# An encoder layer's first stage: modulation by row sums, and two head pairs projected together

## The chip, the cores and the metric

The kernel runs on one core of a Trainium2 chip. TensorE (PE) multiplies matrices, VectorE (DVE), ScalarE (ACT) and GpSimd (POOL) work on tiles of 128 partitions, and SyncE (SP) issues the transfers. The metric is the device time of one execution in microseconds; the figure for a kernel is the median of several runs. A profiled execution of the same kernel shows where the time goes.

## The reference, cut to what matters

One layer of an encoder is computed: batch 1, 2048 tokens of 1024 features, 16 heads of 64. The mixer is stick-breaking attention, and a SwiGLU feed-forward part with 2816 hidden features follows. Everything is float32.

```python
mods = silu(c) @ ada_w + ada_b            # 6 x 1024: shift, scale, gate of the mixer, the same of the FFN
h = rms_norm(x, g) * (1 + scale) + shift  # the input of the mixer
q, k, v = h @ w_qkv                       # the projections, 16 heads each
z = q @ k.T * 64**-0.5                    # then softplus, reverse cumulative sums, exp: the weights a
o = (a @ v) @ w_o                         # the rest of the mixer, then the FFN in the same manner
```

The change concerns the first two and a half of these lines. Only `shift` and `scale` of the mixer are needed before the first projection, that is, the first 2048 of the 6144 columns of `ada_w` (8 MB).

## The kernel before, in words

**Tiles and precision.** The tokens are cut into 4 blocks of 512, the features into 8 tiles of 128 (`KC`), the heads into 8 pairs. A float32 product is made of three matmuls: each factor is split into a high and a low half, and `mm3` (L174 to L178) accumulates high by high (L176), high by low (L177) and low by high (L178). Such a group of three 128x512 matmuls is called a triple here; the projection of a pair and a block has 24 of them (k, q and v, by eight feature tiles), and its pieces are numbered t=1 (k), t=0 (q), t=2 (v) in the order in which they run.

**Steps.** `STEPS` lists the projections (pair, block). The first is (0,0); the second is the *parked* one, (1,0), whose keys, queries and values are stored to memory (`k_park`, `q_park`, `v_park`) and fetched again when pair 1 is due; then (0,1), (0,2) and so on. Attention of pair 0 on block 0 begins once (0,0) is projected and further projections run ahead: `SLICES` counts triples of each step, `AHEAD` says how many are done before the attention's slots begin, and `RATE` spreads the others over the slots.

**Order of work.** PE, ACT, DVE and POOL run in the order in which the program names their operations (`manual_schedule`). SP's order is set by a scheduler. On chip, tiles take turns in a few named groups of places (`ht`, `v`, `kt`, `whl`, `wraw` and so on, counts in `BUFS`), so a tile is loaded only when the tile that had its place has been read.

**The first stage.** The 8 MB of `ada_w` come in four quarters of 256 shift and 256 scale columns (`ada_chunk`). A quarter needs the sum over 1024 rows, each times its element of silu(c). DVE adds up most of the eight row tiles element by element (`ada_sum`: L724 for the first, L727 for each further one, 128x512), PE then sums over the partitions with matmuls against ones whose result is one column (`ada_rest`, L744), and one or two row tiles are multiplied on PE directly with c (`ada_direct`, L737, 128x1 results). `ada_cols_done` (L752 to L755) adds the bias and makes `shift` and `g_eff` = g·(1+scale). Each quarter serves two feature tiles.

Beside it, block 0 of x is squared (ACT, L167), its mean and root are taken (DVE L169, POOL L171), it is scaled (DVE, L341, 128x1024), and transposed feature tile by feature tile (PE, `x_turn`, L372, four 128x128 transposes a tile). `full_high` makes the modulated tile (ACT L782) and its high half (ACT L786), `low` its low half (DVE L791). Weights are split by `weights_high` (ACT L761) and `weights_low` (DVE L766). `first_products` then issues the three triples of a feature tile, for pair 0 alone.

```python
        first_products(m)
        if q < 3:
            turned_x[m + 2] = x_turn(0, m + 2)
            ada_direct(q + 1, KC - 1)
            if q == 0:
                first_products(m + 1, (1,))
            turned_x[m + 3] = x_turn(0, m + 3)
            ada_rest(q + 1)
```

**Block 1.** Blocks 1 and 3 are normalised by features: x comes already transposed from memory (`cols_load`, names `xc`), and what is missing is 1/rms of each token as a row. `x_square` and `x_spread` (L351 for the second) make it per token, `x_share` transposes it on PE (L363) and copies it (L365) to `x_row`. Then, for a feature tile k, `scale_cols` multiplies by that row (even k on DVE, L383; odd k on POOL, L387), and `modulate` makes high and low halves (even k: ACT L400, DVE L401; odd k: ACT L405 and L406, DVE L408). `first_norm` calls both; the scaling runs two tiles ahead. Before the change this lies beside the 24 triples of the parked step: `x_square` of block 1 in its t=1, `x_share` and two calls of `first_norm` in t=0, two more in t=2 (`NORM_AT`). Tiles 4 to 7 are normalised in t=1 of step (0,1), one ahead of each triple.

**Splits and turns.** Each finished projection is copied and split from its PSUM bank: high half by ACT (L507), low half by DVE (names kn and qn). Values are turned on PE (`values_turn`); for the first two steps this is put off, and done in t=1 of a later step (`waiting`). Block 2's x is squared at the places of `SQUARE_AT`, within t=0 and t=2 of the parked step.

Of the kernel before, what the change touches and what calls it, by code (L numbers as in the profile page):

```python
# [16 lines left out]
P = 128  # L17
# [22 lines left out]
SLICES = [0, 3 * KC] + [3 * KC + VGAP] * (NPAIR * NB - 2)  # L40


AHEAD = 6 * KC + 6
# [4 lines left out]

AQ = 256
# [25 lines left out]
SQUARE_AT = [(0, 2), (0, 7), (2, 1), (2, 7)]  # L75

NORM_AT = {
    None: [], 1: [(0, 4), (0, 6), (2, 3), (2, 5)],
    2: [(2, 2), (2, 4), (2, 6)], 3: [(2, 2), (2, 4), (2, 6)],
}  # L80
# [27 lines left out]
def hybrid_trunk_kernel(  # L108
# [5 lines left out]
    ada_first: bass.AP,  # L114
# [28 lines left out]
    shift = const.tile([P, 2, KC], F32, name="shift")  # L143
    c_act = const.tile([P, KC], F32, name="c_act")
# [19 lines left out]
    def rms_scale(pool, src, tag, junk):  # L164

        ssq = pool.tile([P, 1], F32, name=f"{tag}_ssq", tag="rms_ssq", bufs=10)
        nc.scalar.activation(junk, src, AF.Square, accum_out=ssq)  # L167
        ms = pool.tile([P, 1], F32, name=f"{tag}_ms", tag="rms_ms", bufs=4)
        nc.vector.tensor_scalar(ms, ssq, 1.0 / D, EPS, op0=ALU.mult, op1=ALU.add)  # L169
        rstd = pool.tile([P, 1], F32, name=f"{tag}_rstd", tag="rms_rstd", bufs=4)  # L170
        nc.gpsimd.tensor_tensor(rstd, ms, mhalf, op=ALU.pow)  # L171
        return rstd
# [33 lines left out]

    def split_early(p, t, tags):

        raw = raws.pop((p, t))
        if len(tags) == 1:  # L210
            hl = att.tile([P, 2, KC, P], F32R, name=f"w{p}_{t}", tag=tags[0], bufs=BUFS[tags[0]])
            hi, lo = hl[:, 0], hl[:, 1]
        else:
            hi, lo = [
                att.tile([P, KC, P], F32R, name=f"w{p}_{t}_{j}", tag=tag, bufs=BUFS[tag])
                for j, tag in enumerate(tags)
            ]
        nc.scalar.copy(hi, raw)
        nc.vector.tensor_tensor(lo, raw, f32(hi), op=ALU.subtract)
        weights[p, t] = hi, lo  # L220

# [85 lines left out]
    x_tiles, x_norm, x_rstd, x_cols, x_row = {}, {}, {}, {}, {}  # L307

    def x_load(b):
        for i in range(4):  # L310
            r0 = b * BT + i * P
            if b == 2:
                if i % 2 == 0:
                    pair = att.tile([P, 2, D], F32, name=f"x{b}_{i}", tag="qt", bufs=BUFS["qt"])
                tok = pair[:, i % 2]
# [5 lines left out]
    def cols_load(b):  # L321
        for m in range(KC // 2):
# [4 lines left out]
    def x_square(b, i):  # L327
        if b > 0:
# [5 lines left out]
            x_rstd[b, i] = rms_scale(att, tok, f"n0_{b}_{i}", junk=junk)  # L334
# [3 lines left out]
        x_rstd[b, i] = rms_scale(att, x_tiles[b, i], f"n0_{b}_{i}", junk=xn)  # L338
# [38 lines left out]
    def scale_cols(b, k):  # L377
# [4 lines left out]
        if k % 2 == 0:  # L382
# [6 lines left out]
    def modulate(hl, b, k):  # L389

        gain, add = g_eff[:, 0, k : k + 1], shift[:, 0, k : k + 1]
# [7 lines left out]
        if k % 2 == 0:  # L399
# [18 lines left out]
    norm_h, norm_tile = {0: []}, {}  # L418

    def first_norm(b, k):  # L420
# [9 lines left out]
        if k % 2 == 1:  # L430
            nc.sync.dma_start(h_s[b][:, k - 1 : k + 1], f32(norm_tile[b]))
# [21 lines left out]
    def project(at):  # L453

        p, b = STEPS[at]
        begun = (p, b) == (0, 0)
# [7 lines left out]
        def product(t):  # L464
            if begun:
                return first_acc[t]
            w = weights[p, t]
            if parked and t == 1:
                acc = zps.tile([P, BT], F32, name=f"pj{p}_{b}_{t}", tag="z")
            else:  # L470
                acc = accps.tile([P, BT], F32, name=f"pj{p}_{b}_{t}", tag="acc")
            ahead = b == NB - 1 and p + 1 < NPAIR
            for k in range(KC):
                if t == 1:
# [4 lines left out]
                    if k == 5 and waiting:  # L479
                        waiting.pop()()  # L480
                if parked and t == 1 and k % 2 == 0:
                    nc.sync.dma_start(*stores[k // 2])
                if parked and (t, k) == (1, 6):
                    split_early(1, 2, ["whl"])
                if nb in (1, 3) and t == 1 and k < 4:
                    x_square(nb, k)
                if nb and t == 1 and 2 <= k < 6:
                    x_spread(nb, k - 2)
# [6 lines left out]
                if (t, k) in NORM_AT[nb]:  # L495
                    first_norm(nb, NORM_AT[nb].index((t, k)))
# [8 lines left out]
        def split(acc, tag):  # L505
            hl = att.tile([P, 2, BT], F32R, name=f"{tag}n{p}_{b}", tag="qkn", bufs=BUFS["qkn"])
# [25 lines left out]
        if parked:  # L532
            nc.sync.dma_start(q_park, f32(n))
        else:
# [7 lines left out]

# [154 lines left out]
    chunks, piece_sums, cols_ps = {}, {}, {}  # L697

    ON_PE = {0: (0, KC - 1), 1: (KC - 1,), 2: (KC - 1,), 3: (KC - 1,)}

    def ada_chunk(q, kh):
        ks = range(KC // 2 * kh, KC // 2 * (kh + 1))
        if q == 2:
            for k in ks:
                w = att.tile([P, 2, AQ], F32, name=f"ac{q}_{k}", tag="a", bufs=BUFS["a"])
                nc.sync.dma_start(w, ada_first[q, kh][:, :, k % 4])
                chunks[q, k] = w
            return
        tag = "ht" if (q, kh) == (1, 1) else "qt"
        w = att.tile([P, 2, KC // 2, AQ], F32, name=f"ac{q}_{kh}", tag=tag, bufs=BUFS[tag])  # L710
        nc.sync.dma_start(w, ada_first[q, kh])
        for k in ks:
            chunks[q, k] = w[:, :, k % 4]

    def ada_begin(q):
        cols_ps[q] = zps.tile([P, BT], F32, name=f"acol{q}", tag="z")
        nc.vector.memset(cols_ps[q][:, :4], 0.0)

    def ada_sum(q, k):
        w, scale = chunks[q, k], c_act[:, k : k + 1]  # L720
        if q not in piece_sums:
            acc = att.tile([P, 2, AQ], F32, name=f"asum{q}", tag="w", bufs=BUFS["w"])
            piece_sums[q] = acc
            nc.vector.tensor_scalar(acc, w, scale, None, op0=ALU.mult)  # L724
        else:
            acc = piece_sums[q]
            nc.vector.scalar_tensor_tensor(acc, w, scale, acc, op0=ALU.mult, op1=ALU.add)  # L727

    def ada_sums(q):
        return [k for k in range(KC) if k not in ON_PE[q]]  # L730

    COLUMNS = [(2 * seg + j, seg, slice(j * P, (j + 1) * P)) for seg in range(2) for j in range(2)]

    def ada_direct(q, k):

        for n, seg, js in COLUMNS:
            nc.tensor.matmul(  # L737
                cols_ps[q][:, n : n + 1], chunks[q, k][:, seg, js], c_act[:, k : k + 1],
                start=False, stop=False, skip_group_check=True,
            )  # L740

    def ada_rest(q):
        for n, seg, js in COLUMNS:
            nc.tensor.matmul(  # L744
                cols_ps[q][:, n : n + 1], piece_sums[q][:, seg, js], ones[:, 0:1],
                start=False, stop=n == 3, skip_group_check=True,
            )

    def ada_cols_done(q):

        ps, ms = cols_ps.pop(q), slice(2 * q, 2 * q + 2)
        nc.vector.tensor_tensor(shift[:, 0, ms], ps[:, 0:2], b_cols[:, 0, ms], op=ALU.add)  # L752
        sc = att.tile([P, KC], F32, name=f"sc0_{q}", tag="sc", bufs=1)[:, :2]
        nc.vector.tensor_tensor(sc, ps[:, 2:4], b_cols[:, 1, ms], op=ALU.add)
        nc.vector.scalar_tensor_tensor(  # L755
            g_eff[:, 0, ms], sc, 1.0, gc[:, 0, ms], op0=ALU.add, op1=ALU.mult
        )

    def weights_high(t):
        hl = att.tile([P, 2, KC, P], F32R, name=f"w0_{t}", tag="whl", bufs=BUFS["whl"])  # L760
        nc.scalar.copy(hl[:, 0], raws[0, t])  # L761
        weights[0, t] = hl[:, 0], hl[:, 1]

    def weights_low(t):
        hi, lo = weights[0, t]
        nc.vector.tensor_tensor(lo, raws.pop((0, t)), f32(hi), op=ALU.subtract)  # L766

    def first_products(m, ts=(1, 0, 2)):
        for t in ts:
            w = weights[0, t]  # L770
            mm3(
                first_acc[t], (w[0][:, m], w[1][:, m]),
# [3 lines left out]
    def full_high(m):  # L776
        if m % 2 == 0:
            ht = att.tile([P, 2, 2, BT], F32R, name=f"ht0_0_{m // 2}", tag="ht", bufs=BUFS["ht"])
            first_h.extend([ht[:, 0], ht[:, 1]])
            norm_tile[0] = ht  # L780
        full = att.tile([P, BT], F32, name=f"hf0_{m}", tag="tmp", bufs=BUFS["tmp"])
        nc.scalar.activation(  # L782
            full, turned_x.pop(m), AF.Identity,
            bias=shift[:, 0, m : m + 1], scale=g_eff[:, 0, m : m + 1],
        )
        nc.scalar.copy(first_h[m][:, 0], full)  # L786
        first_full[m] = full

    def low(m):
        hl = first_h[m]  # L790
        nc.vector.tensor_tensor(hl[:, 1], first_full.pop(m), f32(hl[:, 0]), op=ALU.subtract)  # L791
        if m % 2 == 1:
            stores.append((h_s[0][:, m - 1 : m + 1], f32(norm_tile[0])))

    nc.sync.dma_start(c_act, c)
    nc.scalar.activation(c_act, c_act, AF.Silu)

# [914 lines left out]
```

## Time and profile before

| what | value |
|---|---|
| runs | 2847.48, 2847.53 and 2849.8 us, median 2847.53 us |
| the profiled execution's own time | 2847.32 us |
| its span, from the first to the last recorded instruction | 2845.3 us |
| busy in the span: PE | 2797.2 us (98%) |
| busy in the span: DVE, ACT, POOL | 2025.0 (71%), 1634.2 (57%), 1288.2 us (45%) |

The profile's page gives busy times of the engines, the span in 40 slices, the chain of waits that ended last, and groups of instructions by line. In such a line the parts are: line of the program, engine, operation, output<-inputs, shapes and types, count (x), then busy time, mean ns of one, idle time ahead of them and what ended it. A timeline row is the start in us, the length in us, and what ran. In the windows each row is one stretch: its bounds and length, the busy us (and count) of PE, PE's weight loads, DVE, ACT and POOL, the granted clock of TensorE (1.00 is full), the mean busy share of the transfer engines, and GB/s.

### The profile page before, as it was taken

To read this page: it belongs to the slowest core of one execution; us is meant where nothing else is said; L and a number is where in the kernel's file an instruction comes from. 1 tells how busy PE (TensorE), PEld (TensorE's weight loads), DVE (VectorE), ACT (ScalarE), POOL (GpSimd) and SP (SyncE) were. 2 spreads that over 40 slices of the span, in tenths; PEclk is the share of its full clock that TensorE was granted. 3 is DMA by queue.
4 is the path that set the end of the run, shared out by engine and by line. 5 is a ranking of instruction groups with operands and counts; after the bars stand their busy time and mean duration, and the time that the engine had idled before them with its cause. 6 is when DMAs were issued, how large, how long until landed. Compare 5 with 4: busy or idle time off the path is not lost.

```text
span 2845.3 us, 41773 instructions
## 1 busy us (share of the span) xinstructions
PE 2797.2 (98%) x13825; PEld 2335.3 (82%) x13825; DVE 2025.0 (71%) x2824; ACT 1634.2 (57%) x3275; POOL 1288.2 (45%) x2036
## 2 busy tenths in 40 slices
PE   8999999999999999999999999999999999999998
PEld 6788888888888888887888788888788888888887
DVE  6788898888888888888866766655776655133376
ACT  5787777788777877777645533333433333322233
POOL 1475666666575655657410122221222222544454
PEclk9999999999999999999999999999999999999999
DMA  9865547657565635646289644334453335545566
GB/s 359 291 219 167 189 151 231 210 170 235 182 211 193 202 123 179 201 127 236 80 304 313 207 137 152 123 94 161 134 175 110 111 105 166 191 139 154 181 212 200
DMA packets 240520, 521.04 MB, mean 183 GB/s; under 512 B 22448, under 2 KB 110512, under 8 KB 222640
## 3 DMA queue, kind: packets, MB, share of 16 engines
q1 hardware_dynamic: 240304, 518.38, 56.1%
q8 instruction: 109, 1.79, 0.3%
q14 instruction: 107, 0.88, 0.1%
HBM read 351.04 MB, written 118.49 MB: 165 GB/s over the span
## 4 chain that ended last, share of the span: by engine, by line
PE 85%; DVE 5%; issue 3%; ACT 2%; POOL 2%; DMA 2%; SPq 0%; DVEq 0%; POOLq 0%; ACTq 0%
PE s L176 9%; PE s L177 9%; PE s L178 9%; PE z L604 8%; PE o L683 8%; PE t L655 8%; PE pj L176 5%; PE pj L177 5%; PE pj L178 5%; PE o L178 4%; PE o L177 4%; PE o L176 4%; PE y L178 2%; PE y L176 2%; PE y L177 2%
## 5 line engine op out<-in xcount | busy, mean ns | idle before, releaser
L645 POOL TENSOR_TENSOR a<-a,w 128x512 f32<-128x512 f32 (+3 forms) x640 | 621.1, 970 | 225.3 <-DVE w L638 130.4
L638 DVE TENSOR_TENSOR_SCAN w<-z,c,begin 128x512 f32<-128x512 f32 x384 | 489.4, 1279 | 84.7 <-ACT z L623 62.1
L176 PE MATMUL s<-r,l 128*128 128x512 f32 x1232 | 481.8, 391 | 4.8 <-DVE p L1447 3.9
L178 PE MATMUL s<-r,l 128*128 128x512 f32 x1232 | 479.9, 389 | 0.0
L177 PE MATMUL s<-r,l 128*128 128x512 f32 x1232 | 479.8, 389 | 0.0
L621 ACT ACTIVATE a<-z 128x512 f32<-128x512 f32 (+3 forms) x640 | 347.1, 542 | 170.7 <-PE z L604 137.6
L683 PE MATMUL o<-aT,v 128*128 128x512 f32 (+3 forms) x1280 | 384.8, 382 | 0.1
L671 DVE TENSOR_TENSOR aT<-t,aT 128x512 fp32r<-128x512 f32 (+3 forms) x640 | 358.8, 595 | 23.7 <-ACT aT L665 23.1
L604 PE MATMUL z<-kt,qt 128*128 128x512 f32 (+3 forms) x1280 | 363.8, 366 | 0.1
L665 ACT CAST aT<-t 128x512 fp32r<-128x512 f32 (+3 forms) x640 | 314.0, 533 | 73.8 <-PE t L655 63.7
L623 ACT ACTIVATE z<-z 128x512 f32<-128x512 f32 (+3 forms) x640 | 345.5, 540 | 0.0
L1455 POOL TENSOR_TENSOR one<-p,p 128x512 f32<-128x512 f32 x44 | 71.5, 1624 | 576.7 <-issue 320.3
L176 PE MATMUL pj<-ht,w 128*128 128x512 f32 x768 | 309.5, 403 | 5.0 <-issue 1.4
L655 PE MATMUL t<-begin,a 128*128 128x128 f32 x2176 | 295.9, 274 | 14.1 <-DVE aT L671 12.9
L655 PEld LDWEIGHTS t<-begin,a 128*128 128x128 f32 x2176 | 255.5, 140 | 64.8 <-DVE aT L671 15.6
L177 PE MATMUL pj<-ht,w 128*128 128x512 f32 x768 | 303.7, 395 | 1.8 <-DVE ht L408 0.6
L178 PE MATMUL pj<-ht,w 128*128 128x512 f32 x768 | 303.3, 395 | 0.0
L176 PEld LDWEIGHTS s<-r,l 128*128 128x128 f32 x1232 | 231.3, 188 | 54.8 <-ACT l L1308 2.9
L178 PEld LDWEIGHTS s<-r,l 128*128 128x128 f32 x1232 | 231.3, 188 | 48.1
L177 PEld LDWEIGHTS s<-r,l 128*128 128x128 f32 x1232 | 231.4, 188 | 47.9 <-issue 0.5
L633 DVE TENSOR_TENSOR_SCAN w<-z,begin 128x128 f32<-128x128 f32 (+3 forms) x256 | 208.8, 818 | 77.0 <-ACT z L623 66.3
L604 PEld LDWEIGHTS z<-kt,qt 128*128 128x128 f32 x1280 | 230.6, 189 | 37.8 <-DVE w L633 0.5
(179 smaller groups left out, 4881.6 us busy)
## 6 DMA issues: line engine op xcount, KB each, us to landing
ht<-h_s SPq DMA_DIRECT2D x108, 1024.0 KB, 8.5
wi<-in_win SPq DMA_DIRECT2D x86, 512.0 KB, 4.0
qt<-qn SPq DMA_DIRECT2D x124, 256.0 KB, 4.9
ol_qt<-act_s SPq DMA_DIRECT2D x56, 512.0 KB, 3.9
act_s<-S SPq DMA_DIRECT2D x66, 256.0 KB, 3.9
br<-in_wout SPq DMA_DIRECT2D x66, 256.0 KB, 3.5
h_s<-ht SPq DMA_DIRECT2D x16, 1024.0 KB, 8.3
o_s<-os SPq DMA_DIRECT2D x128, 128.0 KB, 3.0
```

Of the source, the lines that this page charges most:

```text
L176: nc.tensor.matmul(acc, lhs[0], rhs[0], start=first, stop=False, **kw)
L177: nc.tensor.matmul(acc, lhs[0], rhs[1], start=False, stop=False, **kw)
L178: nc.tensor.matmul(acc, lhs[1], rhs[0], start=False, stop=last, **kw)
L604: nc.tensor.matmul(z[:, :n], q[:, e, part, r * P : (r + 1) * P], k[:, e, :n], start=part == 0, stop=part == 1,)
L621: nc.scalar.activation(a[:, :n], z[:, :n], AF.Sigmoid, scale=QK_SCALE)
L623: nc.scalar.activation(z[:, :n], z[:, :n], AF.Sigmoid, scale=-QK_SCALE)
L638: nc.vector.tensor_tensor_scan(rest[:, rev], left[:, rev], begin[:, :BT][:, rev], initial=carries[r], op0=ALU.mult, op1=ALU.bypass,)
L645: nc.gpsimd.tensor_tensor(a[:, :n], a[:, :n], rest[:, 1 : n + 1], op=ALU.mult)
L655: nc.tensor.transpose(pt[:, rb * P : (rb + 1) * P], weighed[i, rb][:, j * P : (j + 1) * P], ident)
L665: nc.scalar.copy(hl[:, 0, t0:], pt[:, t0:])
L671: nc.vector.tensor_tensor(hl[:, 1, t0:], pt[:, t0:], f32(hl[:, 0, t0:]), op=ALU.subtract)
L683: nc.tensor.matmul(acc[:, t0:], lhs, hl[:, part, t0:], start=sc == qb and j == 0 and part == 0, stop=sc == 0 and j == 3 and part == 1,)
```

## The change

The first stage is written anew; the code from the attention's units on stays as it is.

- **Modulation.** `ada_w` is laid out by feature tile (m = 0 to 7, one half each for shift and scale, 128x1024 each). For m = 0 and 1 (`COLUMNS`) PE makes the column by eight matmuls of 128x1 (`column`). For m = 2 to 7 the transposed rows are loaded, and one DVE instruction multiplies 128x1024 by silu(c) on all partitions and sums along the row (`row_sum`). silu(c) is put on all partitions by two matmuls against ones (`c_over`) and two copies (`c_copy`). `row_done` adds the bias, for one feature tile at a time.
- **Both pairs.** The triples of pair 1 on block 0 (the parked ones) run together with those of pair 0, feature tile by feature tile; pair 1 accumulates in the banks of `zps`. Both steps' products lie in the first stage, `SLICES` is 0 for both.
- **One list.** `FIRST` orders all operations of PE, ACT, DVE, POOL, and the issue of some loads and stores of SP. An entry is a name and its numbers: `sum.ms` half s of tile m, `mod.m` `row_done`, `sq`/`ms`/`sc`.bi square, mean and scaling of x, `xT.m`, `full.m`, `high.m`, `low.m`, `wh`/`wl`.pt the weight halves, `p.ptm` a triple, `sp`/`row` block 1's `x_spread`/`x_share`, `norm.k` `first_norm` of block 1, `c`/`cr` silu(c), `d.` loads and stores.
- **Block 1** is normalised by DVE and ACT alone (odd k too). `norm.0` and `norm.1` stand near the end of the list, calls 2 and 3 come with the splits of step (0,0), 4 to 7 in t=1 of (0,1) as before.
- **Places and SP.** The parked keys and queries are split into places of `wraw` instead of `qkn`; the first two stores of block 1's h wait (`held`) until the parked queries are stored; raw weights of pair 1 load into `v`. Squares of block 2 move to t=0 of (0,1), four in a row; the two waiting turns of values come at k=3 and k=5 of its t=1, oldest first.

The diff, cut to its core:

```diff
+COLUMNS = 2
-SLICES = [0, 3 * KC] + [3 * KC + VGAP] * (NPAIR * NB - 2)
-AHEAD = 6 * KC + 6
+SLICES = [0, 0] + [3 * KC + VGAP] * (NPAIR * NB - 2)
+AHEAD = 3 * KC + 6
...
-        if k % 2 == 0:
+        if k % 2 == 0 or b == 1:
             nc.vector.scalar_tensor_tensor(
                 u, u, g_eff[:, 0, k : k + 1], x_row[b], op0=ALU.mult, op1=ALU.mult
             )
...
-            nc.sync.dma_start(h_s[b][:, k - 1 : k + 1], f32(norm_tile[b]))
+            out_of = h_s[b][:, k - 1 : k + 1], f32(norm_tile[b])
+            if b == 1 and k < 4:
+                held.append(out_of)
+            else:
+                nc.sync.dma_start(*out_of)
...
-        begun = (p, b) == (0, 0)
+        begun = at < 2
...
             if begun:
-                return first_acc[t]
+                if at == 0 and t != 2:
+                    first_norm(1, 2 + (t == 0))
+                return first_acc[p, t]
...
-                    if k == 5 and waiting:
-                        waiting.pop()()
+                    if k in (3, 5) and waiting:
+                        waiting.pop(0)()
...
-                if nb == 1 and (t, k) in SQUARE_AT:
-                    x_square(2, SQUARE_AT.index((t, k)))
+                square_at = {2: 0, 3: 1}.get(nb)
+                if t == square_at and k < 4:
+                    x_square(nb, k)
+                    x_mean(nb, k)
...
         def split(acc, tag):
-            hl = att.tile([P, 2, BT], F32R, name=f"{tag}n{p}_{b}", tag="qkn", bufs=BUFS["qkn"])
+            place = "wraw" if parked else "qkn"
+            hl = att.tile([P, 2, BT], F32R, name=f"{tag}n{p}_{b}", tag=place, bufs=BUFS[place])
...
+    def column(m, seg):
+        w = rows[m][seg].rearrange("p (k f) -> p k f", f=P)
+        out_col = acol[:, 2 * m + seg : 2 * m + seg + 1]
+        for k in range(KC):
+            nc.tensor.matmul(
+                out_col, w[:, k], c_act[:, k : k + 1], start=k == 0, stop=k == KC - 1,
+            )
+
+    def row_sum(m, seg):
+        w = rows[m][seg]
+        if m not in sums:
+            sums[m] = att.tile([P, 2], F32, name=f"as{m}", tag="as", bufs=3)
+        nc.vector.scalar_tensor_tensor(
+            w, w, 1.0, c_rows, op0=ALU.mult, op1=ALU.mult, accum_out=sums[m][:, seg : seg + 1]
+        )
+
+    def row_done(m):
+        total = acol[:, 2 * m : 2 * m + 2] if m < COLUMNS else sums.pop(m)
+        nc.vector.tensor_tensor(mod[:, :, m], total, b_cols[:, 0:2, m], op=ALU.add)
+        nc.vector.scalar_tensor_tensor(
+            g_eff[:, 0, m : m + 1], mod[:, 1, m : m + 1], 1.0, gc[:, 0, m : m + 1],
+            op0=ALU.add, op1=ALU.mult,
+        )
...
+    nc.sync.dma_start(c_act, c)
+    row_load(0)
+    nc.sync.dma_start(c_line[0:1], c_row)
+    x_load(0)
     nc.sync.dma_start(b_cols, ada_b_cols)
     nc.sync.dma_start(gc, g_cols)
+    row_load(1)
+    load_weights(0, 1)
     load_weights(0, 0)
-    load_weights(0, 2, "qkn")
+    load_weights(0, 2, "kt")
+    row_load(2)
+    for t in (1, 0, 2):
+        load_weights(1, t, "v")
+    for m in (3, 4, 5):
+        row_load(m)
...
+    FIRST = """
+        sum.00 sq.00 sum.01 ms.00 sq.01 sq.02 ms.01 sc.00 sq.03 ms.02 sc.01 c mod.0 wh.01 ms.03
+        sc.02 wh.00 wl.01 wh.02 sc.03 d.rows wl.00 xT.0 cr sum.10 wl.02 full.0 high.0 sum.11 sum.20
+        low.0 xT.1 xT.2 mod.1 p.000 sum.21 wh.11 p.010 mod.2 p.020 wh.10 wl.11 full.1 p.110 wl.10
+        full.2 xT.3 high.1 xT.4 sum.30 p.100 high.2 wh.12 low.1 low.2 p.001 p.011 sum.31 p.021 wl.12
+        d.x1a d.xc0 p.101 d.xc1 d.xc2 d.st0 p.111 mod.3 sum.41 p.120 p.121 sum.40 full.3 p.002 p.012
+        high.3 sum.51 p.022 p.102 low.3 p.112 mod.4 p.122 sum.50 p.003 mod.5 p.013 full.4 sum.61
+        p.023 sq.10 p.103 sum.60 d.x1b d.st1 d.x2 high.4 p.113 p.123 sq.11 low.4 xT.5 mod.6 ms.10
+        p.004 full.5 ms.11 sum.71 p.014 sq.12 p.024 sp.10 sp.11 high.5 p.104 ms.12 sum.70 sq.13
+        p.114 p.124 low.5 d.st2 xT.6 ms.13 sp.12 p.005 full.6 mod.7 p.015 sp.13 high.6 p.025 low.6
+        p.105 p.115 p.125 xT.7 d.xc3 p.006 full.7 p.016 high.7 p.026 low.7 d.st3 p.106 p.116 p.126
+        p.007 p.017 p.027 row.1 p.107 p.117 norm.0 norm.1 p.127
+    """
```

More of the change, by code (lines that the diff above doesn't have):

```diff
@@ L47 @@
 EAGER = 12
-AQ = 256
 BUFS = {
@@ new lines, in hybrid_trunk_kernel @@
+    for n in range(4):
+        moves[f"xc{n}"] = lambda n=n: cols_load(1, n)
+        moves[f"st{n}"] = lambda n=n: store(n)
+    begin_do = {
+        "sum": lambda m, seg: (column if m < COLUMNS else row_sum)(m, seg),
+        "mod": row_done, "sq": x_square, "ms": x_mean, "sc": x_scale, "sp": x_spread, "row": x_share,
+        "xT": turn_x, "full": full, "high": high, "low": low, "wh": weights_high, "wl": weights_low,
+        "p": lambda p, t, m: products(p, m, t), "norm": lambda k: first_norm(1, k),
+        "c": c_over, "cr": c_copy,
+    }
```

316 lines of the change are left out of this document (120 added, 196 removed).

## The prediction

> **What bounds the kernel now.** I read the page first, then the windows of the first 160 us, then the timelines of PE, ACT and DVE there, then the groups by form.
>
> ```profile
> span 2845.3 us, 41773 instructions
> PE 2797.2 (98%) x13825; PEld 2335.3 (82%) x13825; DVE 2025.0 (71%) x2824; ACT 1634.2 (57%) x3275; POOL 1288.2 (45%) x2036
> 2.60:20.70 18.10, 8.33 (x33) 6.82 (x33) 9.97 (x19) 9.66 (x16) 3.38 (x4) 1.00 0.98 397
> 20.70:34.20 13.50, 13.42 (x43) 10.97 (x43) 11.25 (x22) 4.25 (x6) 0.00 (x0) 1.00 1.05 387
> 56.50:77.90 21.40, 20.66 (x95) 16.28 (x94) 16.02 (x29) 17.73 (x31) 11.10 (x12) 1.00 1.01 369
> 118.90:160.00 41.10, 34.83 (x178) 27.38 (x177) 34.06 (x44) 35.00 (x74) 33.79 (x54) 0.96 0.62 207
> ```
>
> PE is busy for 2797.2 of 2845.3 us, so whatever PE does not spend, or spends at half clock, is the only thing to win. In the windows (columns: length, then busy PE, PEld, DVE, ACT, POOL, then clock, DMA share, GB/s) PE works 8.33 us of the first 18.10, then nearly always; the next real hole is at 118.9 to 160, 6.3 us, far behind the edit. The DMA share is about 1 at 387 to 397 GB/s, so nothing can be fetched earlier: what is needed first must be asked for first.
>
> ```profile
> 20.70 0.79 PE L176 MATMUL pj<-ht,w 128*128 128x512 f32 x1 [0.67 <-ACT ht L786]
> 22.60 0.63 PE L176 MATMUL pj<-ht,w 128*128 128x512 f32 x1
> 23.02 0.63 PE L177 MATMUL pj<-ht,w 128*128 128x512 f32 x1
> 25.16 1.06 PE L372 MATMUL xT<-begin,xn 128*128 128x128 f32 x4
> 26.00 1.71 PE L737 MATMUL acol<-c_act,ac 128*128 128x1 f32 x8
> 27.57 0.78 PE L176 MATMUL pj<-ht,w 128*128 128x512 f32 x1
> 34.12 0.44 PE L176 MATMUL pj<-ht,w 128*128 128x512 f32 x1
> 35.34 0.39 PE L178 MATMUL pj<-ht,w 128*128 128x512 f32 x1
> 35.56 0.39 PE L176 MATMUL pj<-ht,w 128*128 128x512 f32 x1
> 36.25 0.60 PE L372 MATMUL xT<-begin,xn 128*128 128x128 f32 x4
> 36.69 0.95 PE L737 MATMUL acol<-c_act,ac 128*128 128x1 f32 x8
> 77.25 0.50 PE L177 MATMUL pj<-ht,w 128*128 128x512 f32 x1 [0.28 <-DVE ht L408]
> 77.81 0.39 PE L176 MATMUL pj<-ht,w 128*128 128x512 f32 x1
> ```
>
> Products begin at 20.70 and follow each other every 0.427 us (22.60 to 23.02). From 34.12 they follow every 0.2275 us (35.34 to 35.56). The clock column shows 1.00 all along, yet everything on PE halves there: four transposes 0.84 then 0.44, eight passes of a 128x1 matmul 1.57 to 1.71 then 0.8. So 13.4 us of products ran at half speed. A 128x1 matmul is two passes here (four instructions, eight records): cold about 0.43 us each. At 77.81 step (0,1) begins its second product (t=0); from there both kernels run the same list, so I compare that instant: **before, 77.81**.
>
> **When the first product starts.** Ahead of the first weights the changed kernel fetches row 0, x, row 1: 1.05+2.1+1.05 MB. Before, it was 4.2 MB too, so the weights land as they do now, at 15.24, and the next at 16.63.
>
> ```profile
> 15.24 1.05 ACT L761 CAST w<-wr 128x1024 fp32r<-128x1024 f32 x1 [0.19 <-DMA wr<-in_wqkv]
> 16.63 1.04 ACT L761 CAST w<-wr 128x1024 fp32r<-128x1024 f32 x1 [0.34 <-DMA wr<-in_wqkv]
> 19.22 0.78 ACT L782 ACTIVATE hf<-xT,shift,g_eff 128x512 f32<-128x512 f32 x1 [1.54 <-PE xT L372]
> 20.02 0.62 ACT L786 CAST ht<-hf 128x512 fp32r<-128x512 f32 x1
> 60.30 0.59 ACT L365 COPY x<-xr 128x512 f32<-128x512 f32 x1 [0.38 <-PE xr L363]
> L766 DVE TENSOR_TENSOR w<-wr,w 128x1024 fp32r<-128x1024 f32 x3 | 3.6, 1222 | 0.1
> L727 DVE SCALAR_TENSOR_TENSOR asum<-ac,c_act,asum 128x512 f32<-128x512 f32 x23 | 17.3, 750 | 1.0 <-DMA ac<-in_ada_first 0.4
> L791 DVE TENSOR_TENSOR ht<-hf,ht 128x512 fp32r<-128x512 f32 x8 | 5.5, 690 | 2.5 <-ACT ht L786 2.2
> L755 DVE SCALAR_TENSOR_TENSOR g_eff<-sc,gc 128x2 f32<-128x2 f32 x4 | 0.6, 161 | 0.1
> L341 DVE TENSOR_SCALAR xn<-x,n_rstd 128x1024 f32<-128x1024 f32 x4 | 3.0, 750 | 0.5 <-POOL n_rstd L171 0.4
> ```
>
> In the listed order DVE does wl.01 ahead of sc.03: 15.24+1.05+1.22+0.75 = 18.3, and only then can PE end xT.0. Behind xT.0 on PE stand sum.10 and sum.11, 16 matmuls of 128x1, 32 passes, four rows like 26.00's: 4x1.71 = 6.8 us. Row 1 has landed long before (ahead of 15.24), but the place in the list is behind xT.0, so PE does them at 18.3 to 25.1. Then xT.1 and xT.2, 2x0.84: **first product at 26.8 instead of 20.70**. Nothing covers this: the third weights land at 16.63+0.52/0.397 = 17.9, and ACT has high.0 ready at 17.9+1.05+2x0.59 (cr, as L365)+0.78+0.62 = 21.5, DVE low.0 near 22.2. The early columns sum.00 and sum.01 cost nothing: PE is idle before 18.3, as the 8.33 busy of 18.10 shows. What goes are 36 such matmuls: 12 stood before the first product, the other 24 between the products, 2x1.57 cold + 4x0.8 warm = 6.3 us. About as much as comes in front; the start eats the gain.
>
> **From there to the last product.** Up to p.027 PE has 45 triples, 135 products, 135x0.2275 = 30.7, seven xT and the row transposes, 8x0.44 = 3.5; together 34.2 us at full clock, counted from 25.1. When the clock turns I bound by the one full dip the trace has:
>
> ```profile
> 128.21 0.33 PE L655 MATMUL t<-begin,a 128*128 128x128 f32 x1 [2.28 <-DVE aT L671]
> 129.00:131.00 2.00, 1.98 (x11) 1.44 (x11) 1.76 (x5) 1.53 (x4) 1.51 (x4) 0.69 0.87 279
> 131.00:133.00 2.00, 2.00 (x9) 1.84 (x9) 1.54 (x2) 0.59 (x2) 1.77 (x7) 0.50 0.00 0
> 133.00:135.00 2.00, 2.00 (x13) 1.64 (x12) 0.58 (x1) 1.20 (x2) 1.37 (x2) 0.95 0.00 0
> ```
>
> After a wait of 2.28 us the clock is 0.5 for 1.2+2.0+0.2 = 3.4 us, all busy, then full: decisions come in steps of 3.4 us. At the start no step turned it while columns stood between the products (26.00 to 27.57, and once more); it turned 2.7 us after the last columns. So I count columns as idle and let the clock turn after the first full step of transposes and products from 25.1: between 27.9 and 31.3, I take 29.6. The 4.5 cold us do the work of 2.4: 25.1+34.2+2.1 = 61.4. With the copy of L365 x_row stands at 62.1.
>
> The Trainium skill, "TensorE: Matmul & The Clock Gate", section "What's actually happening", has the clock rise after about 3.4 us of sustained activity. The dip agrees; the 13.4 us at the start do not unless columns count for little.
>
> Can DVE keep up? A row sum, scalar_tensor_tensor of 128x1024 with accumulation, isn't in the trace. The next rows are 1.22 (L766, same size, two tensors) and 0.75 for half the size (L727, same operation). The size costs 0.53 per 512 (1.22-0.69), so 0.75+0.53 = 1.28; I take 1.3. From 20.3 (wl.02 done) to low.5 DVE has 12 sums 15.6, three wl 3.7, six lows 4.1 and some 18 small steps like L755, 3.0: ready by 47 if nothing waits; the listed order makes it wait for sq.12 behind full.5, so about 50. PE reaches low.5 near 50.4 (m=0 to 4 done). Slack under 1 us there, about 5 us at low.3 and low.4, 2 us at low.6 and low.7. sq.13 stands on ACT before full.6 and waits for the fourth x tile, about 18.4 MB into the queue: 2.6+18.4/0.397 = 49; needed by 50.3. On SP the third x1 tile waits for wl.12 and the fourth for sum.60, and st1, x2, st2, xc3, st3 stand behind; nobody needs those before 62. Six row tiles as sums take 12x1.3 = 15.6 of DVE where it spent 28 pieces, 17.3+1.9: off the path either way.
>
> **Step (0,1).** This is the price of doing two pairs together: before, block 1 was normalised beside the 72 products of the parked pair. Now norm.0 starts with x_row, and no product is left to hide it but nine.
>
> ```profile
> L383 DVE SCALAR_TENSOR_TENSOR xc<-xc,g_eff,x 128x512 f32<-128x512 f32 x4 | 2.9, 743 | 0.0
> 62.04 1.41 DVE L383 SCALAR_TENSOR_TENSOR xc<-xc,g_eff,x 128x512 f32<-128x512 f32 x2
> 68.78 0.74 DVE L383 SCALAR_TENSOR_TENSOR xc<-xc,g_eff,x 128x512 f32<-128x512 f32 x1
> 69.44 0.75 DVE L401 SCALAR_TENSOR_TENSOR ht<-xc,shift,ht 128x512 fp32r<-128x512 f32 x1
> L401 DVE SCALAR_TENSOR_TENSOR ht<-xc,shift,ht 128x512 fp32r<-128x512 f32 x4 | 3.8, 951 | 0.3 <-ACT ht L400 0.2
> 78.01 0.59 ACT L507 CAST kn<-pj 128x512 fp32r<-128x512 f32 x1 [1.30 <-PE pj L178]
> ```
>
> Back to back these follow every 0.66 us (68.78 to 69.44). All eight tiles now go by DVE: 8 scalings, 8 low halves, and between them four splits kn, qn, kn, qn (0.61, as L791 less the same overlap): 16x0.66+4x0.61 = 13.0, the last low done at 62.1+13.2 = 75.3. PE ends p.127 near 63.6. It cannot start k=0 before the first kn frees its bank, which stands ninth in DVE's order: 62.1+8x0.66+0.69 = 68.1. So PE stands 4.5 us, drops to half clock by the dip above and turns up a step after it restarts: three triples cold 3.8, a turn of values 0.8, five triples and a turn warm 3.9. t=1 ends at **76.6**. By the mean of L401 (0.95, where POOL multiplies beside it) the chain is 2 us longer; POOL no longer does, so I take 0.66 and keep 2 us for the range. The squares of block 2 moved to t=0 of this step: four of 1.05 on ACT behind kn end at 82, the last scaling at 83.8, where xT of block 2 is wanted at 83.5: 0.3 us lost. The order of SP from here on is as before; the parked stores move less than 8 MB between 68 and 90, which 0.4 MB/us carries before x of block 3 is squared.
>
> **Sum.** 76.6+0.3 against 77.81: -0.9 us. The profiled execution took 2847.32 (span 2845.3 and 2.0 around it), the median of the runs is 2847.53; so **2846.5**. 0.2% is 5.7 us, about what a measurement of this kernel can tell from no change.
>
> **Rivals.**
> *Row sums at half rate* (slower). If accumulation makes DVE read one tensor per cycle, a sum costs 4x0.53+0.22 = 2.35 us. PE takes 4.1+0.44 us for one tile of both pairs, DVE two sums and 1 us: it becomes the bound above 1.75 us a sum. Then low.5 comes at 20.3+12x2.35+10.8 = 59.3, and PE needs 11.1 us from there to the end of the row transposes (two tiles 8.2, three triples 2.05, two turns 0.9): 70.4 for 61.4, with the -0.9 +8.1 us: 2855.6. For it: no row has this operation with accumulation. Against: L727 reads two fp32 tensors at 0.75 per 512, barely over L791's 0.69. The Trainium skill, "Vector Engine (DVE) Microarchitecture Reference", section "Points that are easy to get wrong", says that this operation with two non-bf16 SBUF sources runs at half throughput; L727 disagrees without accumulation.
>
> *Columns warm the clock* (faster). Then PE turns during sum.10, by about 22.7, the rest of the columns takes half and the products never run cold: 24.0+34.2 = 58.2, 3.2 us earlier, -4.1 us: 2843.4; without the dip at 129.8 too (3.4 us at half, 1.6 lost), 2841.8. Against: 26.00 to 27.57.
>
> *The clock stays low as long as before*, 13.4 us from the first product, to 40.2: 10.6 us more at half, +4.9, so +4.0: 2851.5.
>
> **How the numbers follow.** Forecast 0.56, of which its tails give 0.05 faster and 0.03 slower (stalls on DVE or a longer norm chain, -4 to +4); half rate 0.15 (0.13 slower); warm columns 0.18 (0.10 over 5.7 us faster, with the dip gone); long cold 0.11 (0.03 slower, with other stalls). Faster 0.15, slower 0.19, same 0.66. The range reaches to the faster and the slower rival, 2841.8 to 2855.6, leaving out the ends beyond.
>
> **What would show it.** First product at 26.8 with 6.8 us of 128x1 passes in front; row sums of 1.3 us; PE without gaps from 25 to 63; x_row at 62; a hole of 4 us on PE then, with the clock at 0.5; (0,1)'s t=0 from 76.6. Wrong if products start near 22, if a sum takes 2 us, or if PE stands before p.005.

## The result, and the profile after

The changed kernel takes 2850.87 us (median of 22 runs, 2847.95 to 2854.88); the kernel before takes 2847.49 us (22 runs, 2844.23 to 2850.6). The ratio is 1.0014, with a 95% interval of 1.0008 to 1.0020: 3.4 us slower where 1.0 us faster was forecast. It lies in the range given and within 0.2%, but on the other side of zero.

The profiled execution of the changed kernel took 2854.88 us, the longest of its runs, so its span is not compared. What can be compared is when the same instruction starts in the two traces. First the changed kernel's page, and its windows over the stretches shown of the kernel before and those between them (columns as above):

```profile
span 2852.8 us, 41760 instructions
PE 2802.1 (98%) x13821; PEld 2339.9 (82%) x13821; DVE 2024.6 (71%) x2826; ACT 1633.7 (57%) x3274; POOL 1282.9 (45%) x2032
```

```profile
2.60:20.70 18.10, 12.73 (x47) 10.19 (x47) 6.35 (x13) 11.27 (x18) 3.59 (x4) 1.00 1.00 387
20.70:34.20 13.50, 13.50 (x60) 12.36 (x60) 10.22 (x19) 6.96 (x10) 0.00 (x0) 1.00 1.03 409
34.20:56.50 22.30, 22.30 (x105) 18.44 (x104) 15.32 (x39) 9.76 (x17) 3.91 (x4) 1.00 1.03 418
56.50:77.90 21.40, 17.59 (x74) 13.57 (x73) 14.91 (x23) 11.47 (x20) 0.00 (x0) 0.92 0.66 220
77.90:118.90 41.00, 36.89 (x183) 29.30 (x182) 26.90 (x53) 26.57 (x58) 14.91 (x34) 0.96 0.97 334
118.90:160.00 41.10, 34.85 (x177) 27.80 (x176) 33.53 (x45) 34.02 (x72) 32.06 (x48) 0.96 0.65 218
```

PE has no gap from 20.7 to 56.5. It loses 3.8 us between 56.5 and 77.9, about as the prediction said (4.5), and 4.1 us between 77.9 and 118.9, with the clock column at 0.96, where the prediction saw 0.3. The kernel before loses 1.0 us there, at full clock:

```profile
77.90:118.90 41.00, 39.99 (x211) 32.45 (x210) 29.45 (x53) 26.14 (x57) 13.48 (x31) 1.00 0.97 341
```

The timeline of PE in the changed kernel, in order:

```profile
5.17 6.96 PE L716 MATMUL acol<-c_act,ar 128*128 128x1 f32 x32 [5.17 <-DMA ar<-in_ada_cols_first]
19.19 0.48 PE L368 MATMUL xT<-begin,xn 128*128 128x128 f32 x1 [2.80 <-DVE xn L337]
19.46 6.83 PE L716 MATMUL acol<-c_act,ar 128*128 128x1 f32 x32
27.75 0.78 PE L178 MATMUL pj<-ht,w 128*128 128x512 f32 x1
30.88 0.56 PE L179 MATMUL pj<-ht,w 128*128 128x512 f32 x1
31.27 0.40 PE L180 MATMUL pj<-ht,w 128*128 128x512 f32 x1
62.43 0.60 PE L359 MATMUL xr<-begin,x 128*128 128x128 f32 x4
68.86 0.79 PE L178 MATMUL pj<-ht,w 128*128 128x512 f32 x1 [3.74 <-ACT vT L543]
77.46 0.39 PE L178 MATMUL pj<-ht,w 128*128 128x512 f32 x1
86.15 0.33 PE L368 MATMUL xT<-begin,x 128*128 128x128 f32 x1 [1.56 <-DVE x L345]
87.19 0.33 PE L368 MATMUL xT<-begin,x 128*128 128x128 f32 x1 [0.71 <-DVE x L345]
87.86 0.33 PE L368 MATMUL xT<-begin,x 128*128 128x128 f32 x1 [0.34 <-DVE x L345]
88.68 0.33 PE L368 MATMUL xT<-begin,x 128*128 128x128 f32 x1 [0.50 <-DVE x L345]
91.05 1.05 PE L368 MATMUL xT<-begin,x 128*128 128x128 f32 x4
126.64 0.96 PE L652 MATMUL t<-begin,a 128*128 128x128 f32 x7 [1.61 <-DVE aT L668]
```

The row at 77.46 is the start of t=0 of step (0,1); before, it was 77.81, so up to there the change is 0.35 us ahead. Then PE waits four times for the scaled x of block 2, 3.1 us together, and the transposes behind (1.05 at 91.05 where warm ones take 0.60) run at half clock. The last row stands at 121.51 in the trace before, so it is 5.1 us later now:

```profile
121.51 0.96 PE L655 MATMUL t<-begin,a 128*128 128x128 f32 x7 [1.60 <-DVE aT L671]
```

What held the scaled x in the changed kernel is in the timeline of ACT and, in the second block, that of SP (start, length, and the count of moves issued):

```profile
77.70 0.59 ACT L503 CAST kn<-pj 128x512 fp32r<-128x512 f32 x1 [1.21 <-issue]
81.88 1.06 ACT L165 ACTIVATE xj<-x 128x1024 f32<-128x1024 f32 x1 [3.59 <-DMA k_park<-kn]
85.16 1.04 ACT L165 ACTIVATE xj<-x 128x1024 f32<-128x1024 f32 x1
```

```profile
67.02 3.79 SPq L520 DMA_DIRECT2D kt<-kn  x4
71.63 4.76 SPq L536 DMA_DIRECT2D qt<-qn  x4
76.48 0.97 SPq L515 DMA_DIRECT2D k_park<-kn  x1
77.58 1.49 SPq L529 DMA_DIRECT2D q_park<-qn  x1
```

The squares of block 2 write an output that nobody uses (`xj`) into a place of `wraw`. The change put the parked keys and queries into those two places, and the first of them is free only when the store of the keys has landed, 5.3 us after its issue. SP issued that store at 76.48, behind eight moves of the other pair's keys and queries. So the first square, ready at 78.3, began at 81.88.

From 126 us on the lag shrinks: an instruction of ACT near the end of the attention stands at 1402.59 before and at 1405.99 now, 3.4 us, the same as between the medians. The attention gave back 1.7 us in steps of about 0.3, where PE of the kernel before waits for DVE in front of a transpose and the later PE of the changed kernel hardly does (0.38 and 0.10 us at 262 us, 0.24 and 0.00 at 350 us). Behind that the two traces drift apart by about 4 us more, to the spans of 2845.3 and 2852.8; that part isn't explained here.

### The profile page after: what moved, and what is told of

Same layout as the page of the kernel before. It is cut to its first block, busy times and chain, and to the rows that moved or that the text cites. A ratio compares the mean times of both kernels' runs of the same rounds, so it can differ in the third digit from the quotient of the medians.

```text
span 2852.8 us, 41760 instructions
## 1 busy us (share of the span) xinstructions
PE 2802.1 (98%) x13821; PEld 2339.9 (82%) x13821; DVE 2024.6 (71%) x2826; ACT 1633.7 (57%) x3274; POOL 1282.9 (45%) x2032
## 4 chain that ended last, share of the span: by engine, by line
PE 84%; DVE 6%; DMA 3%; issue 3%; ACT 2%; POOL 2%; SPq 0%; DVEq 0%; POOLq 0%; ACTq 0%
PE s L178 9%; PE s L180 9%; PE s L179 9%; PE z L601 8%; PE o L680 8%; PE t L652 8%; PE pj L178 6%; PE pj L180 6%; PE pj L179 6%; PE o L178 4%; PE o L179 3%; PE o L180 3%; PE y L180 1%; PE y L178 1%; PE y L179 1%
## 5 line engine op out<-in xcount | busy, mean ns | idle before, releaser
L668 DVE TENSOR_TENSOR aT<-t,aT 128x512 fp32r<-128x512 f32 (+3 forms) x640 | 358.6, 594 | 24.3 <-ACT aT L662 23.7
```

The costliest lines, as they stand in the source:

```text
L668: nc.vector.tensor_tensor(hl[:, 1, t0:], pt[:, t0:], f32(hl[:, 0, t0:]), op=ALU.subtract)
```

## The experiments

In this table are, for each kernel, three starts on PE in its trace (first product; t=0 of step (0,1); the transposes that stand at 121.51 before), the stretch between the last two, and the medians, each with that of the kernel before run beside it. Each changed kernel has 11 runs, the first one 22, the warm one 10.

| kernel | first product | t=0 of (0,1) | at 121.51 before | stretch between the last two | median us | before | ratio, 95% interval |
|---|---|---|---|---|---|---|---|
| before | 20.70 | 77.81 | 121.51 | 43.70 |  |  |  |
| changed | 27.75 | 77.46 | 126.64 | 49.18 | 2850.87 | 2847.49 | 1.0014 (1.0008 to 1.0020) |
| place of the unused output | 27.74 | 77.39 | 124.07 | 46.68 | 2850.21 | 2846.70 | 1.0012 (1.0003 to 1.0021) |
| row and norms earlier | 27.81 | 72.52 | 120.87 | 48.35 | 2847.03 | 2846.70 | 1.0000 (0.9992 to 1.0009) |
| both | 27.92 | 73.76 | 122.16 | 48.40 | 2845.06 | 2846.70 | 0.9995 (0.9987 to 1.0004) |
| column ahead | 24.38 | 74.01 | 123.18 | 49.17 | 2849.82 | 2846.70 | 1.0010 (1.0001 to 1.0019) |
| both, x of block 3 early | 26.81 | 72.63 | 119.11 | 46.48 | 2843.78 | 2847.62 | 0.9992 (0.9983 to 1.0001) |
| SP's order | 28.36 | 77.61 | 125.56 | 47.95 | 2849.25 | 2847.62 | 1.0012 (1.0004 to 1.0021) |
| warm | 25.30 | 74.99 | 124.06 | 49.07 | 2848.40 | 2847.62 | 1.0008 (0.9999 to 1.0017) |
| all four | 24.00 | 70.17 | 116.47 | 46.30 | 2842.21 | 2847.62 | 0.9986 (0.9977 to 0.9995) |
| all, squares of block 3 later | 24.60 | 70.53 | 116.71 | 46.18 | 2844.15 | 2847.10 | 0.9988 (0.9980 to 0.9997) |
| that, and warm | 22.57 | 70.03 | 118.92 | 48.89 | 2844.49 | 2847.10 | 0.9989 (0.9980 to 0.9998) |

Runs scatter by up to 6 us around their median, so a median of eleven hardly tells 2 us from nothing; the mechanisms are read from the traces. One thing varies there too: the clock turned full between 1.4 and 4.0 us after the first product in kernels whose list is the same that far (29.52, 29.86, 31.27 and 31.88 us in the four with a first product near 27.8), which moves all behind by up to 1.2 us. The stretch from t=0 on is free of that first turn. The clock can also be full for a while before the first product. Of the nine changed kernels with a single product for silu(c), six show it, full from about 15 to 17 us and lost again between 18.2 and 20.5. In the one with x of block 3 early, the first of the 32 column passes still ran at full clock (5.88 us for all, 6.83 in the others with that list), so its first product comes at 26.81: by the clock, not by the edit.

**The place of the unused output.**

```diff
-                junk = att.tile([P, D], F32, name=f"xj{b}_{i}", tag="wraw", bufs=BUFS["wraw"])
+                junk = att.tile([P, D], F32, name=f"xj{b}_{i}", tag="aT", bufs=BUFS["aT"])
```

> The changed kernel, but the squares of block 2 write their unused output into places of aT (free from the last product of pair 1 on) instead of wraw, where the parked keys and queries wait to be stored. Nothing else moves. Theory A (the place: the first square waits 3.6 us for the store of the parked keys): the squares start at 78.3, right behind the copy of kn, the hole on PE at 84 to 89 and the half clock behind it go, and everything from 95 us on comes 4.5 to 5.2 us earlier: about 2846. Rival B (four squares in a row at t=0 come too late by themselves, whatever the place): no change, 2850.9. Rival C (x of block 2 lands late behind the queue of stores): squares start between, gain 1 to 3.

Its timeline of ACT, and in the second block what PE waited for between 77 and 100 us (us in total, times, longest):

```profile
78.11 1.06 ACT L165 ACTIVATE xj<-x 128x1024 f32<-128x1024 f32 x1
81.24 1.05 ACT L165 ACTIVATE xj<-x 128x1024 f32<-128x1024 f32 x1
95.54 1.06 ACT L165 ACTIVATE x<-x 128x1024 f32<-128x1024 f32 x1 [2.13 <-DMA x<-in_x]
```

```profile
PE xT L368 <- ACT hf L390: 2.2, 1, 2.2
PE vt L549 <- ACT vT L543: 0.2, 1, 0.2
```

The mechanism of theory A is shown: the squares start at 78.11, PE has no wait from 77 to 91, and the second tile of block 2 is transposed at 86.33 instead of 91.05. The size is not: the stretch from t=0 takes 46.68 us, 2.5 less than in the changed kernel, of the 5.5 by which that one exceeds the kernel before. PE now waits 2.2 us at 98, because ACT has the squares of block 3 ahead of the modulated tile that PE needs, and x of block 3 lands at 95.5. That wait lay hidden behind the first. The median doesn't show the 2.5 us (1.0012 against 1.0014 for the changed kernel); in this trace the lag against the kernel before is 1.2 us at 1300 us, so they were lost behind that or in the scatter, which stays open.

**SP's order.** The place stays in `wraw`; the eight moves of step (0,0) are named behind the parked stores.

```diff
+            if at == 0:
+                late_moves.append(spread_k)    # spread_q alike
+            else:
+                spread_k()
...
             nc.sync.dma_start(q_park, f32(n))
+            for move in late_moves:
+                move()
```

> The changed kernel with the place in wraw left as it is, but the eight moves of kn and qn of step (0,0) are issued behind the stores of the parked keys and queries on SP. Theory A (the first square waits for the parked store because SP issues it only at 76.5, behind eight moves of 8.6 us, while the keys are split at 72.2): the store leaves near 72.3 and has landed near 77.7, the squares start at 78.3, and the time is that of the kernel with the other place, about 2850 and 2.5 us earlier at 120 us. Rival B (the store itself takes until 82 whatever its turn): as the changed kernel.

```profile
66.65 3.79 SPq L522 DMA_DIRECT2D kt<-kn  x4
71.86 0.33 SPq L516 DMA_DIRECT2D k_park<-kn  x1
73.48 5.08 SPq L545 DMA_DIRECT2D qt<-qn  x4
```

SP's scheduler moved only the four of the queries; that was enough. The store left at 71.86, the first square began at 78.34 without a wait, and PE's four waits are gone. So the wait was SP's turn (the store left 4.6 us sooner), not the store's own time. The stretch from t=0 takes 47.95 us, 1.2 less; the other place brought 2.5. PE waits 2.0 and 1.0 us at 98 to 101 for tiles behind the squares of block 3, as there, and 1.2 us more in front of the scores at 108.9.

**Row and norms earlier, and both.**

```diff
-        ... high.7 p.026 low.7 d.st3 p.106 ... p.017 p.027 row.1 p.107 p.117 norm.0 norm.1 p.127
+        ... high.7 p.026 row.1 low.7 norm.0 norm.1 d.st3 p.106 ... p.017 p.027 p.107 p.117 p.127
```

> The changed kernel, but x_share of block 1 (row.1), norm.0 and norm.1 stand in the list right behind p.026, where DVE has nothing from 58.6 to 63.7, instead of between the last five triples. Theory A (the norm chain of DVE behind x_row is what PE waits for at 65 to 69): the chain starts near 58.7, PE has no hole at 65 and its clock stays full; t=1 of step (0,1) ends near 72.4 instead of 77.5. The wait of block 2's squares for the store of the parked keys stays, but moves along with the splits: 2846. Rival B (the store of the parked keys and the hole of block 2 stand where SP's queue puts them): the 5 us are lost again at 84 to 89, 2850.

> Both edits of the two kernels before. If both waits are as told and independent: -5 and -5, 2841, below the kernel before by 6. If x of block 2 or the next transfer is late next, about 2844.

With the row earlier, t=0 starts at 72.52 instead of 77.46. These are the 4.9 us that were expected, but the sum has other terms. The hole of 3.74 us at 65 and its half clock (another 1.7) are gone, and PE waits 1.54 us at 69 for a low half of block 1 instead, which makes 3.9; the other 0.9 is the clock, full from 29.52 instead of 31.27. With both edits, where the clock was full from 31.88, t=0 moves by 3.7. So most of the price of doing two pairs together was a matter of place in the list. The stretch behind is 48.35, hardly shorter (49.18), since the wait for the parked store moves along, as theory A has it; it is 2.1 us there instead of 3.6. Taking that wait away as well brings nothing there (48.40; t=0 is 1.2 later by the clock alone, full from 31.88 instead of 29.52). The two gains were not independent, against what was expected. With both edits, the largest waits of PE, then of ACT, from 58 to 100 us:

```profile
PE xT L368 <- ACT hf L390: 3.9, 1, 3.9
PE pj L179 <- DVE ht L397: 1.5, 1, 1.5
```

```profile
ACT x L165 <- DMA x<-in_x: 3.8, 1, 3.8
```

The wait for x of block 3 has grown from 2.1 us, with the place of the unused output alone, to 3.8. PE's gap of 3.9 us behind it was followed by half clock from 96.7 to 100, which costs about 1.7 us more and was not there behind the gap of 2.2. Together they take the whole gain.

**x of block 3 early, squares of block 3 later.** First the four loads go ahead of the four moves of kn of step (0,1); then, in the kernel with all edits, the squares come two triples later.

```diff
-                if nb == 2 and (t, k) == (0, 0):
+                if nb == 2 and (t, k) == (1, 6):
                     x_load(3)
...
-                if t == square_at and k < 4:
-                    x_square(nb, k)
+                off = 2 if nb == 3 else 0
+                if t == square_at and off <= k < 4 + off:
+                    x_square(nb, k - off)    # mean and spread alike
```

> The kernel with both edits (place of the squares' output, row.1 and norms early), and x of block 3 loaded in t=1 of step (0,1), ahead of the four moves of kn on SP instead of behind them. Theory A (with the wait for the parked store gone, the squares of block 3 are late next: their four loads leave SP at 85.5 to 90.8, behind v_park and the four moves of kn, 5.5 us, and PE stands 3.9 us at 92 to 96 behind them): the loads leave SP near 79.8 to 84, the hole at 92 goes, and all behind 100 us comes 4 to 5 us earlier than in that kernel: about 2841. Rival B (the transfers are full there, the moves of kn and qn only come later instead): 2844 to 2845.

> The kernel with all four edits so far, and the squares of block 3 on ACT two triples later in t=1 of step (0,2) (k=2 to 5 instead of 0 to 3). In that kernel the first of them waits 2.3 us for x of block 3, although its load left SP at 76.4, and PE stands 2.4 us behind ACT at 91.3. If the wait in ACT's queue is all there is: the hole goes, 2 us less, 2840. If x lands when it lands and the squares only come to stand before later work of ACT: 2842.

The early loads shortened the stretch from 48.40 to 46.48, and PE's wait from 3.9 to 2.3. The loads left SP 6.6 us sooner (78.9 for 85.5) and the first square began 2.8 us sooner (90.79 for 93.55), of which 1.1 is the earlier t=0. The transfers are busy there (share 0.99 to 1.03 from 77 to 100). The half clock behind the gap is in both kernels. With the squares later the hole is gone, the stretch is as long as before (46.18), and a new hole has taken its place: PE waits 2.8 us for the queries of step (0,1), whose moves x of block 3 has overtaken:

```profile
99.98 0.41 PE L602 MATMUL z<-kt,qt 128*128 128x128 f32 x2 [2.82 <-DMA qt<-qn]
```

So from 80 to 100 us the transfers are full, and here the order mostly chose who waits. That fewer bytes in this stretch would help is likely, and no run tested it.

**The column ahead, and all four edits.**

```diff
-        sc.02 wh.00 wl.01 wh.02 sc.03 d.rows wl.00 xT.0 cr sum.10 wl.02 ...
+        sc.02 wh.00 wl.01 wh.02 sc.03 d.rows wl.00 sum.10 xT.0 cr wl.02 ...
```

> The changed kernel, but the first eight column matmuls of tile 1 (sum.10) stand ahead of xT.0 in the list, where PE stands idle from 16.4 to 19.2. Theory A (the columns cost half clock time and do not warm the clock; first product waits for them on PE): first product at 25.1 instead of 27.75, the clock turns 2.7 us earlier too, all kept to the end but for a stall of 0.5 at m=6: -2.2, 2848.6. Rival B (the clock turns at the same instant as now, 31.1): half of it, -1.3. Rival C (DVE or the transfers bind further on): 0.

> The first kernel of this call with the first eight column matmuls of tile 1 ahead of xT.0 as well, which alone brought the first product from 27.75 to 24.4 and x_row by 3.4. If the start is still what sets the end: 3 us below the first kernel of this call, about 2838. If transfers bind from 60 to 100 us: no gain, 2841.

The first product comes at 24.38 instead of 27.75, and the 3.4 us stay to t=0 of (0,1) and to the last landmark; of the medians' ratio they take 0.0004, about 1 us, which is within the scatter. With the other three edits the kernel takes 2842.21 us, 0.9986 of the kernel before (0.9977 to 0.9995). Like the two kernels below it in the table it is faster than the kernel before by more than its interval, and it has the lowest median.

**Warm.** The product that spreads silu(c) is done twice, so PE has wide work from 12 to 17 us.

```diff
-        ... sc.01 c mod.0 wh.01 ms.03
+        ... sc.01 c c mod.0 wh.01 ms.03
```

> The changed kernel, but the two 128x512 products that put silu(c) on all partitions are done twice in a row, so that PE works without a gap on wide products from 12 to 19 us. Asks whether the clock turns there and whether the columns keep it. If columns hold a full clock: sum.10 and sum.11 take 3.4 us instead of 6.8, first product near 24 instead of 27.75, all products at 0.23 us: -4 to -5 in the trace at 60 us. If the clock turns but falls again in the columns: xT.0 late by up to 0.3, products from 27.8 cold again. If it does not turn at all: first product at 28.

> The kernel before this one, with the product that spreads silu(c) done twice, which alone turned the clock at 16 us and brought the first product from 27.75 to 25.3. Theory (a turned clock falls again about 3 us into the columns): sum.10 and most of sum.11 run at full clock, the first product comes near 22 instead of 24, the products cold for 3 us as ever: 2 us less than the kernel before this one, 2838. If DVE is late there (low halves, modulations): less than 1.

In the first of these kernels the eight passes of the doubled product took 5.12 us, where four alone took 3.76: the clock turned in the middle. The timeline of PE, and the windows behind:

```profile
19.34 4.50 PE L716 MATMUL acol<-c_act,ar 128*128 128x1 f32 x32
25.30 0.78 PE L178 MATMUL pj<-ht,w 128*128 128x512 f32 x1
```

```profile
19.50:23.00 3.50, 3.50 (x30) 3.50 (x29) 3.50 (x5) 2.98 (x6) 0.00 (x0) 0.84 1.02 408
23.00:27.00 4.00, 4.00 (x16) 3.71 (x17) 3.15 (x9) 3.51 (x5) 0.00 (x0) 0.50 1.04 413
```

The columns ran at full clock at first, and the clock fell to half at about 21.9 us, after 2.5 us of nothing but columns; a gap of 1.58 us stands ahead of these, so the columns are not alone in question. Together with all other edits there was no such gap: 32 passes in two lots took 3.7 us and the first product came at 22.57. But DVE's low halves were next (0.4 us at 23.4), the clock fell at about 23.7 all the same, and t=0 of (0,1) came 0.5 us earlier; a hole at 99 us and half clock behind it took more than that. The medians expected of the last two kernels, 2840 or 2842 and 2838, were missed (2844.15 and 2844.49).

## Why the prediction was wrong

*The first product* was to start at 26.8 and did at 27.75. The 32 passes took 6.83 us (6.8 forecast); they began at 19.46 instead of 18.3, as the first weights were split from 16.17 on instead of 15.24, and DVE's last scaling of x stands behind them. Why the weights landed 0.9 us later, behind as many bytes, stays open.

*The clock and the way to the row.* Full clock from 31.1 (29.6 taken; 27.9 to 31.3 given), PE without a gap, row transposes ended at 63.0 (61.4). The pitch of 0.2275 us, for which the prediction's two rows give 0.22, held: eight products from 33.30 to 34.91 follow each other every 0.23 us. DVE kept up: a row sum took 1.22 us (1.3).

```profile
L724 DVE SCALAR_TENSOR_TENSOR ar<-ar,c_rows 128x1024 f32<-128x1024 f32 x12 | 14.4, 1218 | 0.0
```

That refutes the rival of half rate, and here the sentence of the Trainium skill, "Vector Engine (DVE) Microarchitecture Reference", section "Points that are easy to get wrong", doesn't hold: two fp32 sources and an accumulated sum cost no more than the two-tensor rows of that size (1.22 us, L766). The rival of warm columns is refuted too: the 6.83 us of columns ran at half clock to their end, and the kernels with the doubled product lost a full clock in or right behind them. So is the rival of a clock that stays low for 13.4 us, since it turned 3.4 us after the first product; that its 2851.5 is close to what was measured is chance.

*Step (0,1)*: a hole of 4.5 us with half clock behind it and t=1 ending at 76.6 was forecast; it was 3.74 us, with half clock, and 77.46. Up to here the sum was off by 0.9 us, and its sign was right: 0.35 us ahead of before. But the wait was not the one named. PE was to go on at 68.1, when the low half of the first kn, ninth on DVE, had freed its bank. It went on at 68.86, right behind ACT's copy of the values, and DVE came to that kn only then:

```profile
68.22 0.59 ACT L543 COPY vT<-pj 128x512 f32<-128x512 f32 x1
68.99 0.69 DVE L504 TENSOR_TENSOR kn<-pj,kn 128x512 fp32r<-128x512 f32 x1
```

So the length of the hole came out by some luck.

*The step that failed* is the sentence on the squares of block 2: "four of 1.05 on ACT behind kn end at 82, the last scaling at 83.8, ... 0.3 us lost", and the one behind it on the stores. The squares lasted as long as said, but from 81.88 to 86.2. The prediction counted ACT's queue and the megabytes, and not the place that the squares write to: it had `wraw` in the diff as the parked pair's new place, and didn't ask who uses `wraw` next. It also counted the parked stores as bytes; what was late was the turn on SP, which took 3.79 us for the first four moves ahead of them and 4.76 us for the next four. Instead of 0.3 us this cost 3.1 us of waits and about 1.7 more at half clock (89.2 to 92.7); 0.7 of the 5.5 by which the stretch is longer stays without a name. Both experiments on it took the wait away; neither gave all of it back, because x of block 3 was next, which the prediction had called covered. In the traces this is shown. In the medians it isn't: with only that wait taken away the kernel is still 1.0012 of the one before, and only the kernels that are 4 us or more ahead of the changed one at the last landmark are clear of it. So the 3.4 us between the medians can't be put down to this wait alone.

*What was not in it*: that the attention gives back 1.7 of 5.1 us by 1400 us.

## What to carry to other kernels

When a change gives a place on chip to other data, list who takes that place next, and when the last reader is done; for a store that is its turn on the issuing queue plus its landing (here 4.6 us lost by the turn and 5.3 from issue to landing), not its bytes over the bandwidth. An output that nobody uses needs a place as well, and can stop an engine. A wait that is taken away pays only up to the next one: find it before pricing the gain.

## What the runs showed of the hardware

Matmuls of 128x1 in a row did not turn TensorE's clock: 32 passes took 6.83 us, at half clock to the end, where 16 take 1.84 at full clock. Nor did they hold it: in the kernel that has all edits and is warm too, PE stood idle for no more than 0.4 us in a row from 11.9 us on, columns took 3.7 of the 5.8 us up to 23.7, and there the clock fell. On SP, in the changed kernel, the four moves at 67.02 took 0.95 us each beside a mean transfer share of 0.30, and the four at 71.63 1.19 us each beside 1.02, so full transfers explain little of that time. Whether a gap costs the clock isn't decided by its length: at 99 us a gap of 2.82 us in one kernel was followed by a full clock, and one of 2.64 us in another by 0.50. The windows behind, first of the kernel with the later squares, then of the one that is warm too:

```profile
100.00:105.00 5.00, 5.00 (x28) 4.35 (x29) 2.68 (x5) 2.13 (x7) 1.89 (x7) 1.00 1.00 410
```

```profile
100.00:105.00 5.00, 5.00 (x17) 4.12 (x17) 1.47 (x4) 1.48 (x5) 1.72 (x5) 0.50 1.01 412
```

The Trainium skill, "TensorE: Matmul & The Clock Gate", section "What's actually happening", says that the window over which activity is judged, about 3.4 us, runs freely. The two gaps agree with that, and so does the turn after the first product, anywhere between 1.4 and 4.0 us.
